# Four more tiles of a down product by Strassen, and a new order for the end of both feed-forward blocks

## The chip, the cores and the metric

The kernel runs on one core of one Trainium2 chip. Its engines are TensorE (PE; its weight loads are listed as PEld), VectorE (DVE), ScalarE (ACT), GpSimd (POOL) and SyncE (SP, which issues loads). The metric is the device time of one execution in microseconds, as the median of several runs; lower is better.

## The reference

One layer of a streaming encoder on 512 tokens of 1024 features, all in float32. Every sub-layer stands between two RMS norms:

```python
f = swiglu(rms_norm(h, g_ffn1_pre[i]), w_ffn1_gate[i], w_ffn1_up[i], w_ffn1_down[i])
h = h + 0.5 * rms_norm(f, g_ffn1_post[i])
u = rms_norm(h, g_mix_pre[i])
qkv = u @ w_in[i]                      # then two kinds of attention, 8 heads each
h = h + rms_norm(mixed @ w_out[i], g_mix_post[i])
f = swiglu(rms_norm(h, g_ffn2_pre[i]), w_ffn2_gate[i], w_ffn2_up[i], w_ffn2_down[i])
h = h + 0.5 * rms_norm(f, g_ffn2_post[i])
e = (p[i] @ w_ple_proj[i]) * jax.nn.sigmoid(h @ w_ple_gate[i])
h = h + rms_norm(e, g_ple_post[i])
```

`swiglu(x) = (silu(x @ w_gate) * (x @ w_up)) @ w_down`, with 2816 hidden features, that is 22 tiles of 128. The change touches the product with `w_down` of both feed-forward blocks, FFN1 and FFN2.

## The kernel before, in words

The state is kept transposed: features on the 128 partitions, tokens along the free axis, so an activation tile is 128x512 and a token half 128x256. To keep float32 accuracy each operand is split in a high part (a copy in a rounded format, by ScalarE) and a low part (the difference, by VectorE; both in `split_to`, L310 to L317, where L312 is the cast and L313 the subtraction of the weights). A product is then three passes: high by high, high by low and low by high (`mm3`, L240, its passes L241 to L243).

Weights stream in chunks of up to 128x1024 (512 KB) through `get` and `ensure`: a chunk is loaded on SP's queue, split, and read by TensorE; splits are issued three chunks ahead (`LOOK`). There are four buffers for split chunks (`wh`, `wl`). Raw chunks have two buffers of one kind (`wr`), three of another (`wx`) and one of a third (`wy`); a load waits until the split of the chunk that had its buffer is done. Chunks can also be split into other, fixed places (`late`).

Hidden tiles 0 to 3 of a block go through plain products. The other 18 make nine pairs, whose gate and up products are done together by a Strassen-like scheme (Winograd's form): seven products instead of eight, each of 24 instructions with 256 columns (`product`, L565). The weight sums that it needs are made by loads that add onto a buffer in place, issued from POOL (`sum_in`, L216); the activation sums are built once (U0 to U6). The seven products run in the order 0, 1, 2, 4, 3, 6, 5 (`ORDER`), alternating between two neighbouring items, so that the evacuation of one lies behind a product of the other. Products 0, 3, 6 and 5 of one item build up in one PSUM bank (tag A), product 1 uses a bank of tag B, and 2 and 4 one of tag z; each tag has two banks.

The down product has four groups of hidden tiles (`GROUPS`, L38): tiles 0 to 3 plain; 4 to 9 and 10 to 15 by the same seven products, as two items each (one per half of the outputs; `down_product`, L616), with 18 instructions per product; and 16 to 21 plain. A down item's product ends with an add of the bank onto the sum `f` (L627). Its activation operands are built by `keep_blocks` (L475); tiles of a plain group are split in `keep` (L499).

The last plain group runs so: two outputs (`e` steps, `begun`, L678) have their products for tiles 16 to 19 put between the last pair's products, and the rest behind them; the other six outputs are done by `tail` (L720), first for the first token half (tokens 0 to 255), six tiles each, and then for the second. Each output's bank is added to `f` and squared into `acc` (`f_out`, L647; ScalarE squares, VectorE adds at L308). `tail(1)` is called from outside (L777, L1097), after `post` has booked the post norm of the first half: the sum over `acc` 13 and the broadcast 20 `mm3` later in FFN1, 14 and 21 in FFN2 (`Q1A`, `Q2A`, L47 and L48), with the residual add, the next norm's gain and the split into `um` (FFN1) or `hs` (FFN2). After FFN1 come the first projections of the mixer (`pj`), which read `um`; after FFN2 come the products of the layer embedding (`pe`), which don't read `hs`, and then the gate products (`pg`), which do.

TensorE's order is the order in the program. For the other engines a planner sets the order of the instructions, and `behind` adds orders by hand; each engine then works its queue in order.

## Time and profile before

| | |
|---|---|
| median of 3 runs | 1005.89 us (1004.18 to 1006.35) |
| span of the profiled execution | 1003.1 us |
| mean granted TensorE clock | 0.998 |
| PE busy, share of the span | 984.5 us, 98% |
| DVE busy | 778.6 us, 78% |
| ACT busy | 590.6 us, 59% |
| POOL busy | 134.1 us, 13% |

The profiled execution is one of its own; its span runs from the first to the last instruction, 2.8 us less than the median of the timed runs. Matmuls overlap in the pipeline, so PE counts as busy also where it isn't at its peak, and the cost of a matmul is read from the distance of starts, not from its duration. A row of busy time by stage gives the stretch, its length, the busy time and instruction count of each engine, the granted clock, the DMA share and GB/s. In the chain of waits a row gives start, length and what the time went to. Names such as `f_dt` are the program's tiles: `f_a`, `f_b`, `f_c` are banks of Strassen items, `f_d` and `f_dt` banks of plain outputs, `f_last0` to `f_last5` the split weight chunks of the last plain group.

### The profile page before, as it was taken

The numbers are of one execution on the slowest core, as the hardware profiler recorded it, in microseconds if no ns is written. First come the engines' busy times: TensorE is split into PE (matmuls) and PEld (weight loads), VectorE is DVE, ScalarE is ACT, GpSimd is POOL, SyncE is SP. The second block draws the span as 40 slices with busy tenths as digits, with TensorE's granted clock in tenths as the row PEclk, the third lists the DMA queues.
The fourth block names the chain that finished last, engine by engine and source line by source line (L and its number), as shares of the span: only waits on it lengthen the run. The fifth ranks groups of instructions, "written<-read, shape, count | busy, mean of one in ns | idle before, by whom it ended". The sixth has DMA issues, their size and how long they took to land.

```text
span 1003.1 us, 18478 instructions
## 1 busy us (share of the span) xinstructions
PE 984.5 (98%) x7242; PEld 924.7 (92%) x7242; DVE 778.6 (78%) x1370; ACT 590.6 (59%) x993; POOL 134.1 (13%) x221
## 2 busy tenths in 40 slices
PE   9999999999999999999999999999999999999996
PEld 7889999999999899888898799889999999999886
DVE  6778777777767788999898868787787777676857
ACT  6446653565356366777789755466554664455563
POOL 0001111212220002334000000012122121210000
PEclk9999999999999999999999999999999999999999
DMA  7348888988886213313423211168889988875102
GB/s 281 102 105 179 171 174 191 187 188 185 201 198 185 99 35 114 95 54 96 125 76 105 86 63 53 53 140 177 193 172 212 188 170 209 188 183 190 61 3 85
DMA packets 44855, 139.71 MB, mean 139 GB/s; under 512 B 5216, under 2 KB 5600, under 8 KB 44768
## 3 DMA queue, kind: packets, MB, share of 16 engines
q0 software_dynamic: 14976, 50.34, 30.2%
q1 hardware_dynamic: 28368, 85.83, 25.3%
q10 hardware_dynamic: 1424, 2.36, 0.9%
q8 instruction: 57, 0.93, 0.4%
q14 instruction: 30, 0.25, 0.1%
HBM read 134.31 MB, written 2.10 MB: 136 GB/s over the span
## 4 chain that ended last, share of the span: by engine, by line
PE 74%; DMA 8%; DVE 8%; issue 5%; ACT 3%; POOL 1%; POOLq 0%; ACTq 0%; DVEq 0%; SPq 0%
PE f_a L241 6%; PE f_a L242 6%; PE f_a L243 6%; PE f_c L242 3%; PE f_c L241 3%; PE f_c L243 3%; PE pj L241 3%; PE pj L242 3%; PE pj L243 3%; DMA wy<-in_wst_dram 3%; DVE wl L313 2%; PE pt L926 2%; DMA wx<-in_wst_dram 2%; PE f_d L242 2%; PE f_d L243 2%
## 5 line engine op out<-in xcount | busy, mean ns | idle before, releaser
L313 DVE TENSOR_TENSOR wl<-wx,wh 128x1024 fp32r<-128x1024 f32 (+1 forms) x104 | 118.3, 1139 | 36.2 <-ACT wh L312 35.1
L312 ACT CAST wh<-wx 128x1024 fp32r<-128x1024 f32 (+1 forms) x104 | 101.8, 984 | 63.3 <-DMA wx<-in_wst_dram 40.8
L313 DVE TENSOR_TENSOR wl<-wr,wh 128x1024 fp32r<-128x1024 f32 (+2 forms) x100 | 109.2, 1098 | 27.2 <-ACT wh L312 27.1
L312 ACT CAST wh<-wr 128x1024 fp32r<-128x1024 f32 (+2 forms) x100 | 94.4, 951 | 44.4 <-DMA wr<-in_wgu_dram 9.8
L216 POOL DMA_DIRECT2D wx<-in_wst_dram x54 | 47.1, 872 | 401.3 <-DVE wl L313 338.0
L312 ACT CAST wh<-wy 128x1024 fp32r<-128x1024 f32 (+1 forms) x52 | 51.3, 986 | 45.9 <-DMA wy<-in_wdst_dram 22.1
L313 DVE TENSOR_TENSOR wl<-wy,wh 128x1024 fp32r<-128x1024 f32 (+1 forms) x52 | 59.2, 1138 | 14.6 <-ACT wh L312 14.6
L241 PE MATMUL pj<-um_hi,wh 128*128 128x512 f32 (+1 forms) x160 | 56.8, 355 | 1.6 <-DVE f_f L648 1.2
L242 PE MATMUL pj<-um_lo,wh 128*128 128x512 f32 (+1 forms) x160 | 55.8, 349 | 0.3 <-DVE um_lo L316 0.3
L243 PE MATMUL pj<-um_hi,wl 128*128 128x512 f32 (+1 forms) x160 | 55.7, 348 | 0.0
L241 PE MATMUL f_a<-f_U6h,wh 128*128 128x256 f32 x144 | 40.2, 279 | 0.9 <-DVE f_x L589 0.9
L243 PE MATMUL f_b<-f_U1h,wl 128*128 128x256 f32 x144 | 40.7, 282 | 0.0
L241 PE MATMUL f_b<-f_U1h,wh 128*128 128x256 f32 x144 | 40.6, 282 | 0.0
L242 PE MATMUL f_b<-f_U1l,wh 128*128 128x256 f32 x144 | 40.6, 282 | 0.0
L241 PE MATMUL f_a<-f_U0h,wh 128*128 128x256 f32 x144 | 40.0, 278 | 0.0
L241 PE MATMUL f_a<-f_U5h,wh 128*128 128x256 f32 x144 | 39.9, 277 | 0.0
L242 PE MATMUL f_a<-f_U6l,wh 128*128 128x256 f32 x144 | 39.9, 277 | 0.0
L242 PE MATMUL f_a<-f_U0l,wh 128*128 128x256 f32 x144 | 39.9, 277 | 0.0
L243 PE MATMUL f_a<-f_U0h,wl 128*128 128x256 f32 x144 | 39.9, 277 | 0.0
L241 PE MATMUL f_c<-f_U4h,wh 128*128 128x256 f32 x144 | 39.9, 277 | 0.0
L242 PE MATMUL f_c<-f_U4l,wh 128*128 128x256 f32 x144 | 39.9, 277 | 0.0
L243 PE MATMUL f_a<-f_U6h,wl 128*128 128x256 f32 x144 | 39.9, 277 | 0.0
(476 smaller groups left out, 3862.6 us busy)
## 6 DMA issues: line engine op xcount, KB each, us to landing
wx<-in_wst_dram POOLq DMA_DIRECT2D x54, 512.0 KB, 5.6
wx<-in_wst_dram SPq DMA_DIRECT2D x18, 512.0 KB, 4.9
wy<-in_wst_dram SPq DMA_DIRECT2D x18, 512.0 KB, 6.1
wr<-in_wst_dram SPq DMA_DIRECT2D x18, 512.0 KB, 5.8
wy<-in_wst_dram POOLq DMA_DIRECT2D x18, 512.0 KB, 5.8
wx<-in_wdst_dram POOLq DMA_DIRECT2D x24, 384.0 KB, 4.9
wr<-in_wqk_dram SPq DMA_DIRECT2D x16, 512.0 KB, 3.7
wr<-in_wgu_dram SPq DMA_DIRECT2D x15, 512.0 KB, 4.4
```

What stands on the lines that cost most here:

```text
L216: pool.dma_start(out=r, in_=block, accum_op=ALU.add)
L241: pe.matmul(ps, hi, mh, start=start, stop=False, skip_group_check=skip)
L242: pe.matmul(ps, hi, ml, start=False, stop=False, skip_group_check=skip)
L243: pe.matmul(ps, lo, mh, start=False, stop=stop, skip_group_check=skip)
L312: a = act.copy(hi, src)
L313: b = dve.tensor_tensor(lo, src, hi.bitcast(F32), ALU.subtract)
L926: pe.transpose(pt[:, qi * P:(qi + 1) * P], aw[qi][:, (j - qi) * P:(j - qi + 1) * P], ident[:])
```

## The change

The plain group 16 to 21 is cut in two. Tiles 16 to 19 become a third Strassen group of two items, x and y, with four tiles: seven products of 12 instructions each, with weight chunks of 128x512. Tiles 20 and 21 stay plain, in 16 pieces, `t` steps, of one output and one token half each (six instructions of 256 columns); their weights come as two 128x1024 chunks, for outputs 0 to 3 and 4 to 7, split to the places of U2 and U4.

The order behind the last pair's last product (`p8.5`) is now: x4, y0, x3, y1, pieces 0 and 1 of the first half, y2, pieces 4 and 5, y4, pieces 2 and 3, y3, pieces 6 and 7; then, after `post` is booked, x6, x5, pieces 4 and 5 of the second half, y6, pieces 0 and 1, y5, pieces 6, 7, 2, 3. Items x and y start between the last pair's products (x0, x1, x2). Products 6 and 5 add to the second token half only. The operands of group 16 to 19 are split in smaller parts, and y's raw buffer for product 4 is the place of U0. The request for the next stage's chunks (`ensure(pos[0] + 3)`) moves behind the tail.

```diff
-GROUPS = ((0, PLAIN), (4, 10), (10, 16), (16, KF))
+GROUPS = ((0, PLAIN), (4, 10), (10, 16), (16, 20), (20, KF))
...
-        for n, step in zip((9, 11, 13), (("e", len(GROUPS) - 1, 0), ("e", len(GROUPS) - 1, 1), ("more", 0, 0))):
-            places[7 * len(items) - 7 + n] = step
-        return [("e", 0, m) for m in range(3)] + [places[i] for i in sorted(places)]
+        late_ops = [places.pop(7 * (len(items) - n) + 2 * i) for n in (2, 1) for i in (5, 6)]
+        for n, m in enumerate((0, 1, 4, 5, 2, 3, 6, 7)):
+            places[7 * len(items) - 5 + 2 * (n // 2) + n % 2 / 2 + 0.25] = ("t", 0, m)
+        steps = [("e", 0, m) for m in range(3)] + [places[i] for i in sorted(places)]
+        (x6, x5, y6, y5), t = late_ops, [("t", 1, m) for m in range(KD)]
+        return steps, [x6, x5, *t[4:6], y6, *t[0:2], y5, *t[6:8], *t[2:4]]
...
+            if kind == "t":
+                if (a, b) == (0, 0):
+                    chunks.extend((w_d[KD + c], 1024) for c in range(2))
...
-                chunks.append((w_dst[b[0] - 1, b[1]], (a, b, 768)))
-        chunks.extend((w_d[len(GROUPS) - 1, m], (GROUPS[-1][1] - GROUPS[-1][0]) * P) for m in range(KD - LAST, KD))
+                chunks.append((w_dst[b[0] - 1, b[1]], (a, b, (GROUPS[b[0]][1] - GROUPS[b[0]][0]) * P)))
...
-            split_to(e4[:, 0], e4[:, 1], w)
-            split_to(e1[:, 0], e1[:, 1], b4[:, 3:4])
+            parts = [(e2, (0, 1)), (e4, (6, 2, 3, 4)), (e1, (5,))]
+            if g == len(GROUPS) - 2:
+                e3, e6 = entries(v0, 1536 * r, 3), entries(v4, 512 * r, 1)
+                split_to(e3[:, 0], e3[:, 1], w[:, 1:4])
+                split_to(e1[:, 0], e1[:, 1], b4[:, 3:4])
+                split_to(e6[:, 0], e6[:, 1], w[:, 0:1])
+                parts[1:2] = [(e3, (2, 3, 4)), (e6, (6,))]
...
-            at_ = [(t, k) for t in range(2) for k in range(2)] + [(t, 2) for t in range(2)]
+            n = (GROUPS[g][1] - GROUPS[g][0]) // 2
+            for t, k in [(t, k) for t in range(2) for k in range(2)] + [(t, k) for k in range(2, n) for t in range(2)]:
...
+        def last_part(hf, m):
+            if not last:
+                last.extend([get(), get()])
+            c0, c1 = HALVES[hf]
+            hi, lo = last[m // 4]
+            ps = psum(("TB" if hf == 0 else "Bz")[m % 2], f"{name}_dt{m}_{hf}")
+            k0, k1 = GROUPS[-1]
+            for k in range(k0, k1):
+                q = slice((m % 4 * 2 + k - k0) * P, (m % 4 * 2 + k - k0 + 1) * P)
+                sh, sl = s[k]
+                mm3(ps[:, c0:c1], hi[:, q], lo[:, q], sh[:, c0:c1], sl[:, c0:c1], k == k0, k == k1 - 1)
             dve.tensor_tensor(f[:, m, c0:c1], f[:, m, c0:c1], ps[:, c0:c1], ALU.add)
-            add_sq(f"{name}_f{m}_{c0}", f[:, m, c0:c1], m == 0, c0, c1)
+            add_sq(f"{name}_f{m}_{c0}", f[:, m, c0:c1], hf not in begun_half, c0, c1)
+            begun_half.add(hf)
...
+        late_raw[base + with_chunk.index(("p", 4, (len(GROUPS) - 2, 1)))] = lambda: unit("ylast", "U0h", 1)
+        n = with_chunk.index(("t", 0, 0))
+        for j, i in enumerate((2, 4)):
+            late[base + n + j] = used(f"last{j}", i)
...
-        last = [get() for _ in range(LAST)]
-        marks.pop("evac")
-        ensure(pos[0] + 3)
-        def tail(hf):
...
-        tail(0)
+        def tail():
+            for kind, x, y in ffn_rest:
+                (product if kind == "p" else last_part)(x, y)
+            marks.pop("evac")
+            ensure(pos[0] + 3)
```

More of the change, by code (lines that the diff above doesn't have):

```diff
@@ L43 @@
 ORDER = (0, 1, 2, 4, 3, 6, 5)
-LAST = 6
 N1, Q1A, Q1B, NMA, NMB = (1, 25, 35), (13, 20), (8, 21), (34, 51), (68, 81)
@@ L212, in emit_split @@
         if add is not None:
-            sum_in(r[:, :n], src[add[0], add[1]])
+            sum_in(r[:, :n], src[add[0], add[1]][:, :n])
     def sum_in(r, block):
         pool.dma_start(out=r, in_=block, accum_op=ALU.add)
-    late = {}
+    late, late_raw = {}, {}
     def ensure(i):
@@ L655, in ffn @@
         base = pos[0] + 2 * (PLAIN - 2)
-        with_chunk = [step for step in ffn_steps if step[0] != "more"]
-        for n, (kind, x, y) in enumerate(with_chunk):
-            if kind == "e" and x and y == 0:
-                late[base + n] = used(f"e{y}", y)
-        for j, i in enumerate((2, 4, 3, 6, 5, 0)):
-            late[base + len(with_chunk) + j] = used(f"last{j}", i)
+        with_chunk = [step for step in ffn_steps if step[0] != "t" or step[1:] in ((0, 0), (0, 1))]
+        late_raw[base + with_chunk.index(("p", 4, (len(GROUPS) - 2, 1)))] = lambda: unit("ylast", "U0h", 1)
+        n = with_chunk.index(("t", 0, 0))
+        for j, i in enumerate((2, 4)):
+            late[base + n + j] = used(f"last{j}", i)
         for m in range(2, PLAIN):
@@ L675, in ffn @@
         f, head = big(f"{name}_f", sa, F32), []
-        def begun(w, ps, g, y):
-            k0, k1 = GROUPS[g]
-            cut = k0 + 2 if g == 0 else k1 - 2
-            if g and y:
-                down(ps, w, g, 0, T, range(k0, k0 + 2))
-                more.append(lambda: down(ps, w, g, 0, T, range(k0 + 2, cut)))
-            else:
-                down(ps, w, g, 0, T, range(k0, cut))
-            return lambda c0=0, c1=T, ks=range(cut, k1): down(ps, w, g, c0, c1, ks)
-        more = []
         for kind, x, y in ffn_steps:
@@ L698, in ffn @@
             if kind == "e":
-                head.append((ps, begun(w, ps, x, y)))
-                if x == 0 and y == 2:
-                    for m, (ps, rest) in enumerate(head):
-                        rest()
+                down(ps, w, 0, 0, T, range(0, 2))
+                head.append((ps, w))
+                if y == 2:
+                    for m, (ps, w) in enumerate(head):
+                        down(ps, w, 0, 0, T, range(2, PLAIN))
                         act.copy(f[:, m, :], ps[:])
-                    head = []
                 continue
```

68 lines of the change are left out of this document (31 added, 37 removed).

## The prediction

> **What bounds the kernel now.** I read the page first, then the chain of waits around the end of the first feed-forward block, then busy time by stage, then single instructions.
>
> ```profile
> span 1003.1 us, 18478 instructions
> PE 984.5 (98%) x7242; PEld 924.7 (92%) x7242; DVE 778.6 (78%) x1370; ACT 590.6 (59%) x993; POOL 134.1 (13%) x221
> ...
> PE 74%; DMA 8%; DVE 8%; issue 5%; ACT 3%; POOL 1%; POOLq 0%; ACTq 0%; DVEq 0%; SPq 0%
> ```
>
> Over the span TensorE is the bound, but this average hides the two places that the change touches, the ends of the feed-forward blocks (FFN1 and FFN2). The chain there, in the first one:
>
> ```profile
> 326.83 5.44 DMA wr<-in_wqk_dram
> 332.35 1.06 ACT wh L312
> 333.43 1.23 DVE wl L313
> ...
> 356.24 0.87 DVE q1b_t L363 x2
> ...
> 367.26 0.41 DVE um_lo L316
> 367.71 0.39 PE pj L242
> ```
>
> For some 40 us the chain runs through VectorE and a weight load, not through the products. Busy time by stage (stretch, length, then PE, PEld, DVE, ACT, POOL with instruction counts): FFN1 from the last pair's fourth gate/up product to the last of `um`; then FFN2 from the same product, with its products' end at 935.6 and the last of `hs` at 957.6.
>
> ```profile
> 298.97:304.30 5.33, 5.33 (x50) 5.33 (x48) 3.80 (x5) 4.29 (x6) 0.86 (x1) 1.00 0.94 166
> 304.30:318.20 13.90, 13.90 (x99) 12.93 (x98) 8.41 (x13) 7.09 (x13) 0.00 (x0) 1.00 0.58 189
> 318.20:330.90 12.70, 12.68 (x111) 12.48 (x110) 11.61 (x18) 7.48 (x12) 0.00 (x0) 1.00 0.70 238
> 330.90:346.30 15.40, 14.38 (x118) 13.78 (x118) 10.92 (x32) 6.71 (x16) 2.27 (x7) 1.00 0.18 60
> 346.30:352.30 6.00, 4.81 (x40) 4.56 (x39) 6.00 (x19) 3.20 (x9) 0.24 (x5) 1.00 0.01 3
> 352.30:367.70 15.40, 14.62 (x127) 14.22 (x125) 14.23 (x49) 8.86 (x23) 0.00 (x0) 1.00 0.01 1
> sum 68.73, PE 65.72 PEld 63.31 DVE 54.98 ACT 37.63 POOL 3.37; mean PE 10.95 PEld 10.55 DVE 9.16 ACT 6.27 POOL 0.56
> ...
> 888.97:894.30 5.33, 5.33 (x49) 5.33 (x48) 2.64 (x4) 3.12 (x4) 0.86 (x1) 1.00 0.93 163
> ...
> 920.90:935.60 14.70, 14.12 (x118) 13.71 (x117) 10.44 (x31) 5.74 (x14) 0.00 (x0) 1.00 0.30 94
> ...
> 942.00:957.60 15.60, 15.60 (x74) 12.93 (x73) 13.15 (x34) 8.46 (x18) 0.00 (x0) 1.00 0.21 68
> sum 68.63, PE 68.05 PEld 62.43 DVE 53.49 ACT 37.63 POOL 0.86; mean PE 11.34 PEld 10.41 DVE 8.91 ACT 6.27 POOL 0.14
> ```
>
> From 346.3 to 367.7 VectorE is busy 20.23 of 21.40 us: here the start of the mixer waits for VectorE. Before that it idles 12.59 us (47.33 less 34.74), and TensorE loses time too, since the norm's sum waits for the squares of the first token half:
>
> ```profile
> 336.86 0.60 PE L255 MATMUL q1a_ss<-ones,acc 128*128 128x1 f32 x4 [0.88 <-DVE acc L308]
> ```
>
> FFN2 ends otherwise: behind it stand the embedding products, which need no normed state, so TensorE goes on at once and the normed second half is ready in time (first and last start in us):
>
> ```profile
> L241 PE MATMUL pe<-wh,wh x16: 389/395/477, 935.7 to 947.0; 128*128 128x512 f32 x16
> ...
> L313 DVE TENSOR_TENSOR hs_lo<-h,hs_hi x16: 416/418/427, 933.6 to 957.1; 128x256 fp32r<-128x256 f32 x16
> ```
>
> The second half is first read after these products (to about 947.7) and 48 gate products of 0.2275 us (price below), at 958.6. So FFN1 is priced by VectorE and FFN2 by TensorE.
>
> **TensorE, part by part.** Prices: twelve 512-column products in 2.73 us, 0.2275 each; 177 256-column ones in 20 us, 0.113 each (gate/up products, no wait).
>
> ```profile
> 304.30:307.03 2.73, 2.62 (x12) 2.18 (x12) 0.00 (x0) 0.00 (x0) 1.00 0.83 317
> ...
> 103.00:123.00 20.00, 20.00 (x177) 20.00 (x177) 15.02 (x20) 11.95 (x17) 3.72 (x5) 1.00 0.83 176
> ```
>
> The last plain group (tiles 16 to 21) costs each block 24 products of 512 columns (two outputs, four tiles, three passes) and 240 of 256 (two outputs, two tiles, two halves: 24; six outputs, six tiles, two halves: 216): 5.46 + 27.12 = 32.6 us. After: two items of seven products, each 4 blocks by 3 passes, 168; and 16 pieces of two tiles, 96. 264 by 0.113 is 29.8 us. Gain 2.75 us per block, 5.5 us in all, if nothing waits.
>
> A rule that speaks against this: the Trainium skill, page "TensorE: Matmul & The Clock Gate", section "Back-to-back issue gap", has sustained products set by weight load and matmul together, 81 ns at 128 columns and 131 at 512, so that narrow products cost more than their share. By my estimate between these, a 256-column product would cost 0.75 of a 512-column one and the gain would halve. By the rule FFN2 below would gain 1.4 us less, and the sum would be 1007.4. The trace disagrees (0.113 against 0.2275), so I don't use it.
>
> **VectorE, part by part.** Its cost is from start to start in a packed run:
>
> ```profile
> 319.12 0.95 DVE L313 TENSOR_TENSOR f_last3l<-wr,f_last3h 128x768 fp32r<-128x768 f32 x1
> 319.99 1.28 DVE L648 TENSOR_TENSOR f_f<-f_f,f_d 128x512 f32<-128x512 f32 x2
> 321.19 2.35 DVE L313 TENSOR_TENSOR wl<-wr,wh 128x1024 fp32r<-128x1024 f32 x2
> 323.46 0.41 DVE L648 TENSOR_TENSOR f_f<-f_f,f_dt 128x256 f32<-128x256 f32 x1
> 323.79 1.22 DVE L313 TENSOR_TENSOR wl<-wr,wh 128x1024 fp32r<-128x1024 f32 x1
> ```
>
> 768 columns 0.87, 512 columns 0.60, 1024 columns 1.13, 256 columns 0.33 us.
>
> Removed per block: eight 768-column weight splits 6.96, one 1024-column split of a pair's activations 1.13, two 512-column adds and one sum of squares 1.80, twelve 256-column adds and twelve sums 7.92: 17.8 us. Added: fourteen 512-column weight splits 8.40, two 1024-column ones 2.26, fourteen 512-column adds behind the Strassen products 8.40, sixteen 256-column adds and fourteen sums 9.90, and the blocks of tiles 18, 19: splits of 512, 768, 256 and 256 columns 2.13 and their differences (512 and two of 256) 1.26: 32.35 us. Net 14.5 us. The like blocks of tiles 16, 17 come earlier and go, with 1.8 us of splits that can move ahead (two of 512 and one of the blocks), into the idle 6.09 us of this row:
>
> ```profile
> 284.00:298.97 14.97, 14.97 (x133) 14.97 (x132) 8.88 (x10) 6.81 (x9) 1.73 (x2) 1.00 0.90 205
> ```
>
> That leaves 12.7 us for 298.97 to 367.7, where VectorE idled 68.73 - 54.98 = 13.75 us. With r us of idle left, the end moves by 12.7 - 13.75 + r = r - 1.05. Bounds for r: 0, and the 8.6% of 318.2 to 330.9 (1.09 of 12.70), 5.9 us. Nearest is the packed stretch 346.3 to 367.7 with 5.5%: r = 3.7. **FFN1: +2.7 us** (-1.05 to +4.9); TensorE's 2.75 us is gone in this, as it then waits for `um`.
>
> **Waits that the change adds.** They price FFN2.
>
> First, the last two weight chunks share the two raw buffers with the items' second weights. The second chunk, which holds output tiles 4 to 7, can be loaded only when the second item's product 1 has its weight split; that split writes where the weights of the last pair's last product lie. ScalarE's queue at that product's end, and the loads' times:
>
> ```profile
> 314.35 0.66 ACT L606 ACTIVATE f_g<-f_a 128x256 f32<-128x256 f32 x2 [3.66 <-PE f_a L243]
> 315.23 0.74 ACT L312 CAST f_sh<-f_b 128x256 fp32r<-128x256 f32 x2 [0.22 <-DVE f_b L607]
> 315.99 1.28 ACT L288 ACT_TABLE_LOAD   x1
> 317.29 0.20 ACT L288 ACTIVATE nx<-eps 128x1 f32<-128x1 f32 x1
> ...
> wr<-in_wqk_dram SPq DMA_DIRECT2D x3, 512.0 KB, 4.3
> ```
>
> After the change the last pair's last product ends at 298.97 + 132 by 0.113 (four gate/up and three down products) = 313.9. The chunk is first read behind 72 more products (four down products, two pieces, one down product: 48 + 12 + 12), at 322.0. Load 4.3, cast 1.06 and subtraction 1.23 (chain rows above) take 6.6 us, so the split must end by 315.4; with the activation and its split ahead of it (0.66 + 0.74) and 1.2 us for itself it ends at 316.5 or later. I take a wait of 1.1 us; bounds 0 and, behind the table load too, 2.6. Queued behind it on TensorE are all later products.
>
> Second, the first item's products 6 and 5 now stand next to each other in one bank: the add between them (0.68 us, as other 512-column adds) lies open. I take 1.0 with the hand-overs; bounds 0.68 and 1.9 (a 1.23 us split ahead of it). Third, between products 2 and 4 of the second item stand only two pieces (1.36 us) for the same add; 0.5 us, from 0 to 2.
>
> FFN2 before takes 935.6 - 888.97 = 46.6 us for 336 products of 256 and 24 of 512. After: 360 of 256, at 0.113 to 0.118 (the row 318.2 has 111 in 12.70, with slips); at 0.115, 41.4 us, and 2.6 us of waits: 44.0. **FFN2: -2.6 us** (40.7 + 0.7 to 42.5 + 6.5: -5.2 to +2.4). VectorE idled 68.63 - 53.49 = 15.1 us there; by the sum above the last eighth of `hs` moves by 12.7 - 15.1 + 3.7 = 1.3 us, to 958.8. TensorE reads it seven eighths into 10.9 us of gate products that would now start at 956.0, at 965.5: hidden, so I add nothing.
>
> The accumulating loads (four per item) and plain loads (three) of 256 KB add 1.6 MB per block. The DMA share from 304 to 346 was 0.70 or less, so I count them as hidden; they cost TensorE if a sum lands late, as each of an item's later weight splits waits for one. On SP's queue the next stage's weights now stand behind buffers that the two items free late; FFN1's first products need four of them, at a point where `um` is late anyway. Moving the prefetch of the next stage's weights behind the tail removes the 5.4 us load from the chain; that is inside VectorE's balance.
>
> **Sum.** On the span: 1003.1 + 2.7 - 2.6 = 1003.2. The span lies 2.8 us under the median 1005.9, so the time is 1006.0 us. What a measurement here can tell is about 0.2%, 2.0 us.
>
> **Rivals.**
>
> - *Both ends gain.* VectorE leaves 0.7 us idle and the waits come to 1.0 us. For it: stretch 346.3 to 352.3 has no idle at all, and the idle before 333.43 came from a load that now moves. Against it: every split needs ScalarE first. FFN1 -0.4, FFN2 41.4 + 1.0 - 46.6 = -4.2: 1005.9 - 4.6 = 1001.3 us.
> - *The last chunk's load, slower.* If the split of the second item's product 1 stands behind the table load or further back, the load starts at 318 or later and TensorE waits 3 us in both blocks, and VectorE, which has only evacuations to do, idles with it. From about 2.3 us of wait it decides. FFN1 2.7 + 1.9, FFN2 -2.6 + 1.9: 1009.8 us. Against it: the splits' order is free until the cast is queued.
> - *VectorE is packed no better than from 318.2 to 330.9* in both blocks: FFN1 +4.9, FFN2 -1.5 as the evacuations lag TensorE by 1.1 us more: 1009.3 us.
>
> **How the numbers follow.** Forecast (no difference to be told, own range 1003.9 to 1007.9) 0.36; both gain 0.34; the load 0.16; packing 0.14. Faster by over 0.2%: 0.34; within: 0.36; slower: 0.30. The range takes the gain to 1000.5, beyond it only where both lower ends meet (-6.3 us), and the slower cases to 1010.5.
>
> **What would show it.** Per block: 360 products from the fourth gate/up product to the end, VectorE about 12.7 us busier; in FFN1 few idle VectorE rows from 300 to 370 and a TensorE wait for `um`; in FFN2 the first embedding product 2 to 3 us closer to the fourth gate/up product; a TensorE wait for the split of the second last chunk near 322, and one before the first item's product 5. The forecast is wrong if VectorE's idle time in FFN1 leaves the bounds of r, or if the first embedding product isn't earlier.

## The result and the profile after

The changed kernel takes 1039.52 us (median of 5 runs, 1036.10 to 1040.59) against 1005.89 us for the kernel before (median of 5 runs beside it, 1004.18 to 1008.94): the ratio is 1.0335, with a 95% interval of 1.0314 to 1.0356. The forecast was 1006.0 us, so it is wrong by 33.5 us, far more than its range allows. The page of the changed kernel begins so, and the shares of the chain of waits stand last:

```profile
span 1034.4 us, 18659 instructions
PE 993.3 (96%) x7242; PEld 932.1 (90%) x7242; DVE 811.8 (78%) x1444; ACT 601.5 (58%) x1025; POOL 147.5 (14%) x237
...
PE 80%; DVE 8%; issue 5%; DMA 4%; ACT 2%; POOL 1%; POOLq 0%; DVEq 0%; ACTq 0%
```

TensorE executes the same number of instructions, 8.8 us busier (984.5 to 993.3) and 22.5 us more idle (1003.1 - 984.5 = 18.6 to 1034.4 - 993.3 = 41.1). So there are two losses, waits and slower products; the second was nowhere in the prediction. (In the changed kernel and its variants the code of `mm3` stands some lines lower: its passes are L247 to L249, the cast L318, the subtraction L319, the accumulating load L222, the add behind a down item L640.)

Busy time by stage of the changed kernel, as before from the last pair's fourth gate/up product (296.27) to the last of `um`, and in FFN2 from the same product (903.98) to the first gate product (979.0). Columns are stretch, length, PE, PEld, DVE, ACT, POOL, granted clock, DMA share, GB/s:

```profile
296.27:311.00 14.73, 12.54 (x111) 12.37 (x110) 12.36 (x19) 9.20 (x14) 2.29 (x3) 1.00 0.79 157
311.00:325.00 14.00, 12.19 (x86) 11.59 (x86) 8.55 (x16) 4.96 (x10) 2.60 (x3) 0.88 0.56 124
325.00:340.00 15.00, 10.82 (x88) 10.24 (x87) 11.67 (x25) 7.20 (x14) 4.71 (x7) 1.00 0.78 196
340.00:352.20 12.20, 10.80 (x91) 10.41 (x90) 11.30 (x28) 6.89 (x13) 0.18 (x3) 1.00 0.44 129
352.20:370.60 18.40, 12.93 (x69) 12.53 (x68) 14.80 (x43) 7.48 (x19) 0.23 (x5) 0.72 0.19 58
370.60:382.00 11.40, 11.26 (x98) 11.06 (x96) 10.71 (x35) 6.39 (x16) 0.00 (x0) 1.00 0.01 1
sum 85.73, PE 70.53 PEld 68.19 DVE 69.39 ACT 42.12 POOL 10.01; mean PE 11.76 PEld 11.37 DVE 11.56 ACT 7.02 POOL 1.67
...
958.40:979.00 20.60, 15.48 (x59) 12.07 (x58) 14.23 (x41) 9.26 (x21) 0.00 (x0) 0.83 0.26 78
```

FFN1's stretch is 85.7 us where it was 68.7. VectorE does 14.4 us more in it (54.98 to 69.39), about the 12.7 that were predicted, and idles 16.3 us (85.73 - 69.39), where the prediction left it 3.7. The granted clock is 0.88 and 0.72 in two of the stretches, and 0.83 under FFN2's embedding products; before it was 1.00 throughout.

From the starts of the products, the ways that the prediction priced, and the two stretches behind them, compare so:

| us | before | after |
|---|---|---|
| FFN1, fourth gate/up product to the mixer's first product | 47.3 | 56.0 |
| mixer's first product to its first v product (`pj` to `pv`) | 26.8 | 35.2 |
| FFN2, fourth gate/up product to the first embedding product | 46.8 | 54.4 |
| first embedding product to the first gate product (`pe` to `pg`) | 11.9 | 20.6 |

The four differences are 8.6, 8.4, 7.6 and 8.7 us, 33.3 in all. (The start of FFN1's fourth gate/up product lies anywhere from 295.4 to 300.6 us in the sixteen traces, though most edits lie behind it, so its 2.7 us here mean nothing.) Below, "way" is the first or third row.

TensorE's waits on FFN2's way, changed kernel (before there was one, 0.5 us, for the norm's sum):

```profile
PE f_a L247 <- DVE f_y L608: 2.2, 1, 2.2
PE f_a L247 <- DVE f_f L640: 1.2, 1, 1.2
PE f_a L247 <- ACT wh L318: 1.0, 1, 1.0
PE f_dt L247 <- ACT f_last1h L318: 0.9, 1, 0.9
PE f_dt L249 <- DVE f_last1l L319: 0.8, 1, 0.8
PE f_b L249 <- DVE wl L319: 0.7, 1, 0.7
```

With three of 0.7, 0.3 and 0.2 they make 8.1 us before rounding; in FFN1 it is 9.6. First of all stands the last pair's last product (p8.5 from here on), which the prediction did not have waiting. The chain of waits of the changed kernel says where that comes from, and what the stretch behind it hangs on:

```profile
307.21 1.05 ACT wh L318
308.29 1.07 DVE wl L319
309.43 0.68 DVE f_sl L319
310.11 0.60 DVE f_y L608
...
312.87 0.86 POOL wx L222
313.74 6.60 issue
320.36 0.86 POOL wx L222
321.22 4.13 issue
325.36 4.47 DMA wx<-in_wdst_dram
329.87 1.75 issue
331.63 5.76 DMA wx<-in_wdst_dram
338.87 0.61 DVE f_f L640
```

Casts, subtractions and accumulating loads, one behind the other, until item x's add between products 6 and 5. (`issue` is time for which this view names no cause; GpSimd's own rows name a subtraction, `wl` L319, as what its loads at 320.36 and 325.36 waited for.) The product itself is slow after its wait. Three stretches of the changed kernel, the wait, p8.5's 24 products (and one more), and the next products:

```profile
308.50:310.90 2.40, 0.21 (x3) 0.07 (x1) 2.40 (x4) 1.31 (x3) 0.00 (x0) 1.00 0.40 55
310.90:315.30 4.40, 4.40 (x25) 4.40 (x26) 1.61 (x3) 0.00 (x0) 1.73 (x2) 0.61 0.65 163
315.30:318.00 2.70, 2.70 (x25) 2.70 (x24) 1.85 (x5) 2.27 (x5) 0.00 (x0) 1.00 0.66 101
```

25 products in 4.40 us at a granted clock of 0.61, and then 25 in 2.70 at 1.00. The same at the wait for the second half's squares in FFN2:

```profile
964.80:970.00 5.20, 0.25 (x2) 0.00 (x0) 5.20 (x14) 3.21 (x8) 0.00 (x0) 0.99 0.28 87
970.00:976.00 6.00, 5.92 (x16) 4.85 (x17) 1.43 (x9) 1.84 (x4) 0.00 (x0) 0.50 0.03 12
```

### The profile page after: what moved, and what is told of

It reads as the page before. It is cut to its first block, busy times and chain, and to the rows that moved or that the text cites. A ratio compares the mean times of both kernels' runs of the same rounds, so it can differ in the third digit from the quotient of the medians.

```text
span 1034.4 us, 18659 instructions
## 1 busy us (share of the span) xinstructions
PE 993.3 (96%) x7242; PEld 932.1 (90%) x7242; DVE 811.8 (78%) x1444; ACT 601.5 (58%) x1025; POOL 147.5 (14%) x237
## 4 chain that ended last, share of the span: by engine, by line
PE 80%; DVE 8%; issue 5%; DMA 4%; ACT 2%; POOL 1%; POOLq 0%; DVEq 0%; ACTq 0%
PE f_a L247 7%; PE f_a L248 7%; PE f_a L249 7%; PE f_c L247 4%; PE f_c L249 4%; PE f_c L248 4%; PE pj L247 3%; PE pj L248 3%; PE pj L249 3%; DMA wx<-in_wdst_dram 2%; PE f_b L247 2%; PE f_b L249 2%; PE f_b L248 2%; PE pt L925 2%; DVE wl L319 2%
## 5 line engine op out<-in xcount | busy, mean ns | idle before, releaser
L319 DVE TENSOR_TENSOR wl<-wx,wh 128x1024 fp32r<-128x1024 f32 (+2 forms) x120 | 129.3, 1079 | 41.4 <-ACT wh L318 40.2
L318 ACT CAST wh<-wx 128x1024 fp32r<-128x1024 f32 (+2 forms) x120 | 111.8, 936 | 77.2 <-DMA wx<-in_wst_dram 33.1
L319 DVE TENSOR_TENSOR wl<-wr,wh 128x1024 fp32r<-128x1024 f32 (+2 forms) x102 | 110.2, 1085 | 21.2 <-ACT wh L318 21.1
L318 ACT CAST wh<-wr 128x1024 fp32r<-128x1024 f32 (+2 forms) x102 | 95.6, 940 | 40.9 <-DMA wr<-in_wgu_dram 10.8
L222 POOL DMA_DIRECT2D wx<-in_wst_dram x54 | 47.1, 872 | 402.7 <-DVE wl L319 196.1
L318 ACT CAST wh<-wy 128x1024 fp32r<-128x1024 f32 (+2 forms) x56 | 53.8, 960 | 40.0 <-DMA wy<-in_wdst_dram 26.0
L319 DVE TENSOR_TENSOR wl<-wy,wh 128x1024 fp32r<-128x1024 f32 (+2 forms) x56 | 61.9, 1105 | 10.0 <-ACT wh L318 9.9
L248 PE MATMUL pj<-um_lo,wh 128*128 128x512 f32 (+1 forms) x160 | 57.9, 362 | 2.6 <-DVE um_lo L322 2.6
L247 PE MATMUL pj<-um_hi,wh 128*128 128x512 f32 (+1 forms) x160 | 58.6, 366 | 0.0
L249 PE MATMUL pj<-um_hi,wl 128*128 128x512 f32 (+1 forms) x160 | 57.7, 361 | 0.0
L222 POOL DMA_DIRECT2D wx<-in_wdst_dram x36 | 31.2, 868 | 112.1 <-DVE wl L319 99.8
L247 PE MATMUL f_a<-f_v,wh 128*128 128x256 f32 x160 | 44.5, 278 | 1.9 <-ACT wh L318 1.9
L247 PE MATMUL f_a<-f_U5h,wh 128*128 128x256 f32 x144 | 41.4, 288 | 4.4 <-DVE f_y L608 4.4
L249 PE MATMUL f_a<-f_v,wl 128*128 128x256 f32 x160 | 44.5, 278 | 0.5 <-DVE wl L319 0.5
L248 PE MATMUL f_a<-f_v,wh 128*128 128x256 f32 x160 | 44.3, 277 | 0.0
L248 PE MATMUL f_a<-f_U5l,wh 128*128 128x256 f32 x144 | 41.2, 286 | 0.0
L249 PE MATMUL f_a<-f_U5h,wl 128*128 128x256 f32 x144 | 41.2, 286 | 0.0
L249 PE MATMUL f_b<-f_U1h,wl 128*128 128x256 f32 x144 | 40.7, 282 | 0.0
L247 PE MATMUL f_b<-f_U1h,wh 128*128 128x256 f32 x144 | 40.6, 282 | 0.0
L247 PE MATMUL f_a<-f_U6h,wh 128*128 128x256 f32 x144 | 40.0, 278 | 0.3 <-DVE f_x L602 0.3
L247 PE MATMUL f_a<-f_U0h,wh 128*128 128x256 f32 x144 | 40.0, 278 | 0.0
```

The lines of the kernel that those rows point to most:

```text
L222: pool.dma_start(out=r, in_=block, accum_op=ALU.add)
L247: pe.matmul(ps, hi, mh, start=start, stop=False, skip_group_check=skip)
L248: pe.matmul(ps, hi, ml, start=False, stop=False, skip_group_check=skip)
L249: pe.matmul(ps, lo, mh, start=False, stop=stop, skip_group_check=skip)
L318: a = act.copy(hi, src)
L319: b = dve.tensor_tensor(lo, src, hi.bitcast(F32), ALU.subtract)
```

## Experiments

Rows and ways are those of the one profiled execution of each kernel. Three theories stood at the start: VectorE's added work (VectorE theory); weight sums, loads and casts that stand late in a queue and hold what is behind them (queue and load theories); and the clock, which falls after a wait. Ratios are to the kernel before on the same chip, with their 95% intervals; the changed kernel's is 1.0335.

**Raw buffers of their own for the two last chunks**

```
+            late_raw[base + n + j] = lambda j=j: unit(f"rawlast{j}", ("U0l", "U3h")[j], 1)
```

> The two weight chunks of tiles 20 and 21 get raw buffers of their own (the low part of U0's place and the high part of U3's), so their loads no longer wait for a buffer that an item's weight split frees; nothing else changes. Queue theory (a cast that waits for such a load holds everything behind it in ScalarE's queue, and with it VectorE's evacuations): the waits of 2.2 us for f_y before the last pair's last product and of 1.4 us for the second chunk go in both blocks, and that product takes 2.7 us where it took 4.4. In FFN2 that is 5.3 us off the way from the fourth gate/up product to the first embedding product (54.4 to about 49.1); in FFN1 between 0 and 5.3, as VectorE's queue for um may then decide: 1029 to 1034 us. VectorE theory (its 14.5 us of added work a block are the cause, the loads only show where): the waits come back behind other VectorE work, FFN2's way stays within 1.5 us of 54.4, and the time is 1037 us or more.

Ratio 1.0327 (1.0289 to 1.0364), no change; ways 57.3 and 55.4 us. The wait for the second chunk is gone, p8.5's stays:

```profile
310.69 0.36 PE L250 MATMUL f_a<-f_U5h,wh 128*128 128x256 f32 x1 [2.24 <-ACT wh L321]
```

In the changed kernel ScalarE stood 3.1 us in front of the first chunk's load just there, which had looked like the cause. With the load out of the way the product waits as long. That reading of mine fell.

**Products 6 and 5 of an item apart**

```
-        return steps, [x6, x5, *t[4:6], y6, *t[0:2], y5, *t[6:8], *t[2:4]]
+        return steps, [x6, y6, x5, *t[4:6], y5, *t[0:2], *t[6:8], *t[2:4]]
```

> Behind the norm's booking the order is x6, y6, x5, pieces 4 and 5, y5, and then the other six pieces of the second half: products 6 and 5 of one item no longer stand next to each other in one bank. Hand-over theory (the wait between them is the add and its place in VectorE's queue): the waits before x5 (2.8 us in FFN1, 1.2 in FFN2) fall under 0.5 each, FFN2's way to the first embedding product falls by 1.0 to 1.6 us, FFN1's by up to 3: 1036 to 1038 us. VectorE theory: the waits move to the next bank (y5 or the pieces) and the time stays within 1 us of 1039.5.

Ratio 1.0362 (1.0324 to 1.0400), if anything slower; ways 60.0 and 57.7. The wait before x5 went in FFN2 but stayed at 2.1 us in FFN1, and others came back at the second chunk (2.2 and 2.0 us) and at the first half's sums (2.6 and 2.3), which the pieces now reach later.

**TensorE kept busy ahead of p8.5**

```
+            if op == 5 and p == PAIRS - 1:
+                fill = psum("T", f"{name}_fill")
+                for _ in range(20):
+                    pe.matmul(fill[:, :HT], hi[:, :P], uh[:, 0, :], start=True, stop=True)
```

> 20 products of 256 columns into a free bank (2.3 us at full clock) stand before the last pair's last product in both blocks, where TensorE waits 2.2 us for f_y; their result is read by nobody. Clock theory (the wait of 2 us brings the granted clock down to about half for the next 3 us or so, so that the 24 products behind it take 4.4 us): the 24 products take 2.7 to 2.9 us, the granted clock behind them stays at 0.95 or more, FFN2's way falls by 1.5 us and the time by 1.5 to 3.4. Rival (the 24 products were slow for their operands, late splits between them): they still take 4 us or more, and the time rises by 0 to 1 us.

Ratio 1.0340 (1.0304 to 1.0377). The stretch that holds p8.5's 24 products (313.79 to 316.63, 2.84 us):

```profile
314.00:318.00 4.00, 4.00 (x37) 4.00 (x37) 2.29 (x5) 0.95 (x3) 1.72 (x2) 1.00 0.69 176
```

The clock stays at 1.00 and the product is 1.6 us shorter, as the clock theory has it. The time gains nothing: the second chunk's wait grew from 0.7 and 0.8 us to 2.5 and 0.8 in FFN1.

**The second half's sums later**

```
-N1, Q1A, Q1B, NMA, NMB = (1, 25, 35), (13, 20), (8, 21), ...
-QMA, QMB, N2A, N2B, Q2A, Q2B = ..., (14, 21), (9, 14)
+N1, Q1A, Q1B, NMA, NMB = (1, 25, 35), (13, 20), (17, 30), ...
+QMA, QMB, N2A, N2B, Q2A, Q2B = ..., (14, 21), (17, 22)
```

> The norm's sum over the second half's squares stands 17 groups of three products behind its booking in both blocks (before 8 in FFN1, 9 in FFN2), the broadcast 30 and 22 (before 21 and 14). In FFN2 the wait of 5.0 us at that sum goes, and with it the slow embedding products behind it. Clock and place theory: from the first embedding product to the first gate product 20.6 us become 12 to 13, and the time falls by 5 to 8.5 us unless the gate products then wait for hs. VectorE theory: hs is as late as before, the gate products wait for it, and the time falls by less than 3. In FFN1 the wait of 3.1 us at the sum goes, but the mixer's second half needs um from the same chain: 0 to 2 us.

Ratio 1.0260 (1.0198 to 1.0321): the largest gain of a single edit that leaves the products and their order as they are and computes the whole result. From the first embedding to the first gate product:

```profile
957.00:968.20 11.20, 11.20 (x51) 8.94 (x50) 11.13 (x28) 7.79 (x18) 0.00 (x0) 1.00 0.42 129
```

11.2 us where it took 20.6, at full clock: 5.0 us of wait are gone and 4.4 of the rest, 3.4 of which the granted clock accounts for (0.50 for 6.8 us in the changed kernel). VectorE does as much work over the span as before the edit (812.0 us). The gate products took 1.5 us more. In FFN1, where the mixer needs `um`, the gain is 2.5 us (35.2 to 32.8).

**Fewer squares**

```
-            add_sq(f"{name}_f{m}_{c0}", f[:, m, c0:c1], hf not in begun_half, c0, c1)
+            add_sq(...) if hf not in begun_half else None
```

> Left out: behind the pieces of tiles 20 and 21 only the first output of each token half is squared into the norm's sum; 14 squares of ScalarE and 14 adds of VectorE (0.33 us each, 4.6 us a block) are gone, so the post norm's scale isn't the reference's. VectorE theory (VectorE's amount of work sets both ends): FFN2's way from the fourth gate/up product to the first embedding product falls by 4 us or more (54.4 to 50.4 or less), FFN1's from the same place to the mixer's v products by 4.6 or more beside the wait at the second sum. Queue and load theory (TensorE waits for weight sums and splits that stand late in a queue, VectorE idles meanwhile): FFN2's way falls by 2.5 at most, the part of the waits that stands behind a square (x5: 1.2, the first sum); only the waits at the second half's sums (3.1 and 5.0 us, with the slow products behind them) go, as they do with later sums: 1022 to 1031 us.

Ratio 1.0189 (1.0146 to 1.0231). VectorE is 9.4 us less busy (802.4), but the ways are 56.5 and 58.3 us, not shorter; all that is gained lies at the second half's sums (`pj` to `pv` 28.7, `pe` to `pg` 13.4). The trace is of an execution of 1028.3 us; the other three took 1019.2 to 1021.7, and what they did on the ways no trace shows. In the one that was traced TensorE's waits on the ways are 8.7 and 9.3 us, where they were 9.6 and 8.1. So VectorE's amount of work isn't what lengthens the ways here. It is among what makes the second sums late; but the squares left out are also what these sums read, so the run doesn't tell the amount of work from their own lateness.

**Splits ahead of p8.5's evacuation**

```
+                if p == PAIRS - 1:
+                    ensure(pos[0] - 1 + LOOK)
```

> The splits that are asked for at the last pair's last product, x3's among them, go into the queues ahead of that product's evacuation instead of behind it, the table load included. Queue theory: x3's split is done while the last product runs; the waits of 0.9 and 0.2 us before and in x3 and of 0.7 us in y1 go in both blocks, FFN2's way falls from 54.4 to about 52.6, FFN1's by 0 to 1.8: 1035 to 1038 us. Load theory (the next weight sum or chunk is late anyway): the waits come back at y1, at the second chunk or at y2 and the way stays within 0.7 us of 54.4. VectorE theory: the same.

Ratio 1.0321 (1.0291 to 1.0350), no difference that counts; ways 56.5 and 53.1. The waits before x3 and in y1 are gone in both blocks; the one before x5 is 4.7 us where it was 2.8 (3.3 where it was 1.2 in FFN2). ScalarE's queue in this kernel, ahead of it:

```profile
331.48 0.62 ACT L318 CAST wh<-f_ylast 128x512 fp32r<-128x512 f32 x1 [1.66 <-DMA f_ylast<-in_wdst_dram]
332.01 0.41 ACT L313 ACTIVATE f_f_sq<-f_f 128x256 f32<-128x256 f32 x1
335.30 0.62 ACT L318 CAST wh<-wx 128x512 fp32r<-128x512 f32 x1 [2.88 <-DMA wx<-in_wdst_dram]
335.82 0.41 ACT L313 ACTIVATE f_f_sq<-f_f 128x256 f32<-128x256 f32 x1
```

A cast of y's weights waits for its sum and holds a square. In VectorE's queue an add waits for that square, and behind it stands the add that x5 needs (L642):

```profile
336.27 0.43 DVE L314 TENSOR_TENSOR acc<-acc,f_f_sq 128x256 f32<-128x256 f32 x1 [2.19 <-ACT f_f_sq L313]
336.61 0.75 DVE L675 TENSOR_TENSOR f_f<-f_f,f_dt 128x256 f32<-128x256 f32 x2
337.27 0.42 DVE L314 TENSOR_TENSOR acc<-acc,f_f_sq 128x256 f32<-128x256 f32 x1
337.61 0.68 DVE L642 TENSOR_TENSOR f_f<-f_f,f_a 128x512 f32<-128x512 f32 x1
```

This is a blocked queue, at another place than I had it. The changed kernel has the same order before x5: its chain above goes from the load at 331.63 to the add at 338.87.

**The natural order of x6, x5, y6, y5**

```
-        late_ops = [places.pop(7 * (len(items) - n) + 2 * i) for n in (2, 1) for i in (5, 6)]
-        return steps, [x6, x5, *t[4:6], y6, *t[0:2], y5, *t[6:8], *t[2:4]]
+        return steps, [("t", 1, m) for m in (0, 1, 4, 5, 2, 3, 6, 7)]
-(13, 20), (8, 21)
+(4, 10), (8, 21)
```

> The second half's products are not put last: x6, x5, y6, y5 stand in the natural order between y's other products, and behind the booking of the first half's norm come only the eight pieces of the second half; the norm's sum and broadcast in FFN1 stand 4 and 10 groups of three products behind the booking (before 13 and 20). Hand-over theory: the wait before x5 goes, FFN2's way falls by 1.2 to 2.5 us from 54.4; in FFN1 the broadcast now stands 2.0 us of products ahead of the mixer where it stood 5.4, so the mixer waits 3 to 6 us more for um: in sum 1038 to 1043 us. Rival, VectorE theory: the adds of x5 and y5 come earlier and VectorE is free sooner, both ends gain, 1036 us or less.

Ratio 1.0297 (1.0260 to 1.0333). FFN1's way is 5.1 us longer, `pj` to `pv` 6.1 shorter, FFN2's way the same (54.2), `pe` to `pg` 4.5 shorter. The expected gain on FFN2's way didn't come, since y's products 6 and 5 are now neighbours and wait 3.3 us in FFN1 and 1.7 in FFN2; the gain is at the second sums, as the squares are done earlier. Putting the second half's products last seems to have cost more than it brought: the gain is 0.4%, the two intervals just touch, and the first half's sums moved with it.

**Three edits in one** (own buffers, later sums, splits ahead)

> Raw buffers of their own for the two chunks, the second sums later (17 groups of three), and x3's split ahead of the evacuation, in one kernel. If the waits are independent: 9.3 us from the sums, 1.8 us a block from x3 and y1, 1.4 us a block from the second chunk: 1018 to 1023 us. If each wait taken away comes back at the next load or queue: the gain of the later sums alone, 1026 to 1031 us.

Ratio 1.0253 (1.0224 to 1.0281), ways 54.5 and 55.0: the gain of the later sums alone. Waits on the ways don't add up; each that goes makes room for the next.

**Splits asked for two chunks ahead**

```
+NEAR = 2
-            ensure(pos[0] - 1 + LOOK)
+            ensure(pos[0] - 1 + (NEAR if p == PAIRS - 1 else LOOK))
```

(and likewise behind x's and y's products and for the two last chunks)

> From the last pair's last product on, splits are asked for two chunks ahead, not three, so that a cast that waits for a weight sum stands less far in front in ScalarE's queue. Blocked-queue theory: the squares and adds behind such casts run earlier; the wait before x5 falls from 2.8 to under 1 us in FFN1 and from 1.2 to under 0.6 in FFN2, x3's split runs later or equally late; FFN2's way to the first embedding product falls from 54.4 to between 52.5 and 53.8. Load theory (sums and chunks land too late for products of 1.4 us each): the splits themselves are now late, waits for a chunk come before x3, y1, y2 or y3, and the way is 54.4 us or longer.

Ratio 1.0343 (1.0306 to 1.0380); ways 60.9 and 57.4. The splits themselves are late now: `f_y`'s wait in FFN1 is 3.2 us (1.4 in FFN2), the one before x3 2.0 and 2.3. Asking later doesn't help, as the load theory has it.

**All five long waits filled**

The edit of the run with p8.5 filled, and such products also ahead of x5 (22 and 11), of the mixer (20) and of the second sums (27 and 44), by

```
+    def busy(ps, w, x, n):
+        for _ in range(n):
+            pe.matmul(ps, w, x, start=True, stop=True)
```

> Products of 256 columns whose result nobody reads fill TensorE's five long waits: 20 before the last pair's last product, 22 (FFN1) and 11 (FFN2) before x5, 20 before the mixer's first product, 27 and 44 before the second half's sums. Clock theory: no stage falls to 0.5 or 0.7 of the clock any more, each filled wait costs what it did, and the slow products behind it go: 1.6 us a block at the last pair's last product, about 1.2 at the mixer's first products, 1.4 to 2.6 behind the sum in FFN1, 3.0 to 3.6 behind the one in FFN2; the time falls by 5 to 9 us, or less where the next wait takes it up. Rival (the slow products are slow for another reason, operands or contention with VectorE): the granted clock or the time of these products doesn't change, and the time rises by 0 to 3 us.

Ratio 1.0222 (1.0178 to 1.0266): 1.1% faster than the changed kernel by 164 products that compute nothing. The stages that had been slow:

```profile
312.00:316.00 4.00, 4.00 (x36) 3.95 (x35) 2.89 (x5) 0.19 (x1) 1.62 (x2) 1.00 0.53 141
...
364.00:368.00 4.00, 4.00 (x36) 3.91 (x35) 3.44 (x14) 2.30 (x8) 0.00 (x0) 1.00 0.00 0
...
972.00:976.00 4.00, 4.00 (x21) 3.38 (x20) 1.54 (x5) 1.71 (x4) 0.00 (x0) 1.00 0.00 0
```

These stretches had 26, 21 and 11 products in the changed kernel; the mean clock is 0.998 where it was 0.987. TensorE is busy for 1001.6 us, less 164 by 0.113 = 18.5 for the fillers 983.1: against 993.3 the slow clock cost 10.2 us by this estimate. The fillers take about as long as the waits did, so what is saved is the slow products behind them.

**Natural order and later sums**

> The natural order of x6, x5, y6, y5 (as in the run before with it, sum and broadcast of the first half 4 and 10 groups behind the booking) and the second half's sums later (14 and 26 groups of three behind the booking in FFN1, 17 and 22 in FFN2). If both gains are of their own, the embedding products take 11.5 to 12 us where they took 16.1, FFN1's mixer stretch 27.5 where it took 29.1, and the time is 1026 to 1029 us. If the sums' place only mattered because of the late order: no change from 1033 us.

The sums at (14, 26) in FFN1 and (17, 22) in FFN2. Ratio 1.0244 (1.0197 to 1.0292); `pe` to `pg` 11.4 us, but the gate products 3.0 us longer, and FFN1 nearly as in the natural order alone. By the ratio it lies between the two expectations.

**No weight sums for x and y**

```
-        if add is not None:
+        if add is not None and item[0] != len(GROUPS) - 2 or add is not None and len(item) == 1:
```

> Left out: the four accumulating loads each of items x and y in both blocks (2 MB a block); their products read the weight blocks without the sums, so the output isn't the reference's. Loads theory (TensorE's waits between the last pair's fourth product and the next stage come from weight sums that land 5 to 7 us behind their issue, and from casts that stand waiting for them in ScalarE's queue): the last pair's sums land sooner, casts no longer wait, x5's wait falls under 1 us; FFN2's way falls from 54.4 to 50 or less. Queue-order theory (splits stand behind evacuations by the order of issue, wherever their data is): the waits for f_y, before x3 and in y1 stay within 0.5 us, and the way stays at 52 to 54.4.

Ratio 1.0236 (1.0200 to 1.0272); ways 52.2 and 53.1. The waits for `f_y`, before x3 and in y1 are the same to 0.1 us in FFN1, and x5's falls to 0.9: so leaving out the new items' own sums is worth 1.3 to 3.8 us a block (1.5 of the latter because p8.5 happens to run at full clock in FFN1), and p8.5's wait isn't due to them. It hangs on the last pair's sum, whose accumulating load is issued at 300.01 in the changed kernel and takes 7.1 us (in the row the label of the releaser, a product that ended in that moment, misled me). It lands at 307.10, and the cast starts 0.1 us later; in FFN2 it is the same, 914.87 and 914.97:

```profile
296.96 1.04 ACT L318 CAST wh<-wx 128x1024 fp32r<-128x1024 f32 x1
...
300.01 0.89 POOL L222 DMA_DIRECT2D wx<-in_wst_dram  x1 [3.21 <-DVE wl L319]
...
307.20 1.05 ACT L318 CAST wh<-wx 128x1024 fp32r<-128x1024 f32 x1 [0.79 <-PE f_a L248]
```

From the cast of product 3's weights to that of product 5's it is 10.2 us. Before, the products from the start of product 3 to that of product 5 took 9.6 us (301.69 to 311.28); with x's shorter steps between them it would be 8.2 (72 by 0.113). The chain itself was shorter before, 8.4 us from cast to cast, with 1.4 us less for the load:

```profile
296.93 1.05 ACT L312 CAST wh<-wx 128x1024 fp32r<-128x1024 f32 x1
...
305.34 1.06 ACT L312 CAST wh<-wx 128x1024 fp32r<-128x1024 f32 x1 [0.79 <-DMA wx<-in_wst_dram]
```

So the time between the products fell by 1.4 us and the chain grew by 1.8. With the chain of before the wait would be about 0.2 us by this sum; that is an estimate, and no run tried it.

**y's product 1 ahead of p8.5**

```
+        places[7 * len(items) - 9.5] = places.pop(7 * len(items) - 5)
```

> Product 1 of item y (12 instructions, 1.36 us) stands ahead of the last pair's last product instead of behind x3; nothing else changes. Weight-sum theory: the chain of the last pair's sums (split of product 3's weights, an accumulating load of 7.1 us, cast and subtraction) takes 10.2 us, the products between the starts of products 3 and 5 only 8.2; with 1.4 us more of other work the wait for f_y falls from 2.2 to between 0.5 and 1.2 us, too short for the clock to fall, and the last product takes 2.7 to 2.9 us in both blocks: 3.0 us a block less up to its end, and FFN2's way 51 to 53.5 us unless a later wait takes it back. Order theory (f_y stands behind the split in VectorE's queue, wherever the split's data is): f_y comes later with the work that moved ahead of it and the wait stays at 2 us or more.

Ratio 1.0278 (1.0244 to 1.0313). The first instructions of p8.5:

```profile
311.74 0.36 PE L248 MATMUL f_a<-f_U5h,wh 128*128 128x256 f32 x1 [0.20 <-DVE f_y L609]
...
312.78 0.38 PE L250 MATMUL f_a<-f_U5h,wl 128*128 128x256 f32 x1 [0.57 <-DVE wl L320]
```

The wait for `f_y` is 0.2 us, another 0.6 stands before the first `wl`, and no slow product follows. The chain still takes 10.2 us, and the products between now 9.5: this is the weight-sum theory's reading, against the order theory's. The ways are 55.4 and 53.5, the latter at the long end of the expectation, since 1.8 and 2.6 us before x5 remain and 2.9 at the first sum in FFN1 is new.

**Four edits together** (y's product 1 ahead; natural order with two pieces between y's products 6 and 5; sums later)

> Product 1 of y ahead of the last pair's last product, natural order but for y's product 5, which stands behind the first two pieces of the second half, sum and broadcast of the first half 4 and 11 groups of three behind the booking in FFN1, those of the second half 14 and 26 in FFN1 and 17 and 22 in FFN2. If the gains add up (3 us a block from the last pair, 3 us a block from the hand-over between y's products 6 and 5, 2 to 4 from the sums beyond the natural order): 1015 to 1022 us, still slower than before. If each wait taken away comes back later: 1026 us or more.

Ratio 1.0212 (1.0183 to 1.0240), 1027.7 us: the fastest version with the change that computes the whole result, still 2.1% slower than the kernel before. It is the second expectation that came, each wait taken away comes back later. The ways are 56.2 and 52.9, with waits of 1.7 to 2.6 us for adds of other products and for the squares of the first half's sum. No version tried, with the whole result or without, beats the kernel before.

## Why the prediction was wrong

**Price and count of the products: the count right, the price of FFN2's way too low.** There are 360 products on a way, and 25 take 2.70 us where the clock is full. But the prediction set 41.4 us of bare products against a measured 46.6 before, which held the norm's instructions and small slips. At full clock, in the run with all waits filled, FFN2's way is 52.0 us; less 3.9 of waits and 31 fillers (3.5) that is 44.6. So by this estimate 3.2 us of the way were left out of the forecast "-2.6" for FFN2. The Trainium skill's rule on narrow products (page "TensorE: Matmul & The Clock Gate", section "Back-to-back issue gap"), which the prediction rejected, would not have helped: by it the sum was 1007.4.

**VectorE's work: right in amount, wrong in what it does.** 14.4 us more in FFN1 for 12.7. The step that failed is r, the idle time that VectorE keeps: put at 3.7 us with bounds of 0 and 5.9, measured 16.3. With 16.3 in its place FFN1's own sum gives the 17.0 us that the stretch grew by. I took r from stretches in which VectorE was hardly short of work (5.5% idle). Here its work is released piece by piece by weight sums, casts and TensorE itself: in 311 to 325 it is busy 8.55 of 14.00 us. With 9.4 us of its work gone, 4.7 a block, the traced ways got no shorter.

**Waits: the three named ones near their size in part, the list wrong.** The second chunk's load: 1.1 predicted, 1.4 and 1.7 measured. x5: 1.0 predicted with 1.9 at most, 2.8 and 1.2 measured. y's products 2 and 4: 0.5 predicted, none found. FFN2 was given 2.6 us of waits, and had 8.1. One failing sentence is that the DMA share was 0.70 or less, "so I count them as hidden": without x's and y's own sums the ways were 3.8 and 1.3 us shorter. The larger part, p8.5 (2.2 us), doesn't come from them. Its own chain (cast, subtraction, accumulating load) takes 10.2 us against 8.2 us of products; the prediction counted x's shorter steps as time saved, and didn't ask what they leave the last pair's sum. What stands behind (x3, y1, the norm's broadcast: 3.2 and 2.9 us) was missing too.

**The second half's sum: taken as hidden.** The prediction asked when TensorE first reads `hs`; the sum over its squares stands 9 groups of three into the embedding products, in TensorE's own order, and there TensorE waits. The prediction quoted the first half's such wait (0.9 us) and didn't ask for the second's. These waits are 3.1 and 5.0 us. Later sums take both away, but in FFN1 the mixer then waits 2.4 us more for `um`.

**The clock: not in the sum at all.** Each product was priced at full clock, whatever stands before it. It cost 10.2 us of the 31.3 us of span by the run with all waits filled. The granted clock in the changed kernel's trace agrees: within the four stretches it is 0.50 for 23.9 us, which costs 11.9 us at most.

As an account of the whole, by estimate: waits of 0.15 us and more in the four stretches of the table come to 28.4 us where they were 3.4, 25.0 more; the half clock costs up to 11.9; and the products saved are 5.5. That is 31.4 of the 33.3 us by which these stretches grew.

**Rivals.** The load rival had VectorE idle with TensorE, which happened, but by another trigger: with the chunk's load out of the way the time didn't move. The packing rival had VectorE idle too, but up to 5.9 us where it was 16.3. The rival in which both ends gain (1001.3) fell with r. None of the prices (1009.8, 1009.3, 1001.3) came near, since none let one wait bring the next, or a wait slow the products behind it.

Not settled: what the best version still loses. Its waits are for adds that stand behind other work in VectorE's queue, 1.4 us of products apart; no run tried a different order of that queue. Nor is it settled why the last pair's accumulating load became slower.

## What to carry to other kernels

Before products are made shorter, compare the time between two uses of a chain (load or sum, cast, subtraction) with the chain's latency, row by row; a mean share of an engine or of the DMA doesn't show it. Allow for the chain to grow, too: here it went from 8.4 to 10.2 us. Price a wait of TensorE of 2 us or more with the slow products behind it, and put sums over late data where the data is ready, since TensorE waits in its own order. Where a wait can't be removed, products that compute nothing can pay for themselves; here all five places together did, and the one before p8.5 alone did not.

## What was unexpected of the hardware

In the stretches around the two ends, of all sixteen traces, TensorE's gaps that stand alone (no other of 1 us or more within 3 us) had 2 us or more of half clock within the 5 us behind them in 11 of 65 cases when they were 1 to 2 us long, in 38 of 50 at 2 to 3 us, and in 16 of 17 above. The same gap does it or not: without the weight sums of x and y, p8.5 waits 2.2 us as in the changed kernel, and runs at full clock.

The granted clock in the traces shows why. In each of the sixteen, every stretch of half clock starts on one grid of 3413 ns and lasts a whole number of its steps, one to four, but for the last, which the end cuts off. By that grid, a step at full clock in which TensorE was idle for less than 45% was never followed by half clock (none of 4587); idle for more than 55%, it always was (76 of 76); between, in 8 of 26 cases. The wait before p8.5 falls into one step of the changed kernel, which has 1.22 us of 3.41 busy, and the next step is slow:

```profile
307.72:311.13 3.41, 1.22 (x11) 1.05 (x10) 2.84 (x4) 2.09 (x4) 0.00 (x0) 1.00 0.51 86
311.13:314.54 3.41, 3.41 (x18) 3.41 (x17) 1.38 (x3) 0.00 (x0) 1.73 (x2) 0.50 0.57 156
```

Without the weight sums the same wait lies across two steps, each of which stays more than half busy:

```profile
305.33:308.74 3.41, 2.43 (x22) 2.23 (x20) 2.32 (x3) 2.54 (x5) 2.07 (x4) 1.00 0.28 91
308.74:312.16 3.42, 2.21 (x19) 2.24 (x20) 2.87 (x5) 0.16 (x1) 0.01 (x1) 1.00 0.54 159
310.00:312.90 2.90, 2.90 (x25) 2.90 (x26) 1.60 (x3) 0.00 (x0) 0.00 (x0) 1.00 0.48 164
```

So a gap of 2 us slows what follows or not by where it falls on the grid, and the grid lies differently in each trace. That is what the Trainium skill, page "TensorE: Matmul & The Clock Gate", section "What's actually happening", has: the clock is either full or half, by activity in a window of 3413 ns that runs freely; the trace agrees, with the 0.50 of the row at 970 and the grid above. The section "HAM oscillation — how this bites in real kernels" of that page asks for no idle gap above about 3.4 us; here 2 us were enough in most cases, and the measurement decides.

An accumulating load of 512 KB from POOL took 5.7 us before, and 7.1 at the same place in the changed kernel and in the runs looked at there (own buffers, p8.5 filled, splits ahead, no sums), each time with a plain load of 512 KB issued beside it; before there was none. That one slows the other wasn't tried apart.
